# A four-layer decoder step: all convolution pairs from the fourth block on by seven products, with half of one low part made by an adding transfer

## The chip, the cores and the metric

The program runs on one core of a Trainium2 chip, in one launch. The metric is device microseconds, the median of several runs. Engines are named as in the profile: PE (TensorE), ACT (ScalarE), DVE (VectorE), POOL (GpSimd), and SP, which only issues transfers. PEld is PE's weight load.

## What is computed

One inference step of four layers, for 512 prompt tokens and 8 sample tokens that share all weights (520 columns; the model width is 1024). Each layer has another token mixer; the change is in layer 1, the gated short convolution:

```python
def shortconv_mixer(h, w_in, conv_w, w_out, buf):
    u = h @ w_in
    bg, cg, xb, z = jnp.split(u, 4, axis=-1)
    cx = cg * xb
    ...
    out = (bg * y * jax.nn.silu(z)) @ w_out
```

Here `w_in` is 1024 x 8192, so each of the four parts has 16 row blocks of 128. All arithmetic is float32 in effect.

## The kernel before

**Products in two halves.** Every weight tile (128 x 1024, 512 KB) is split into a high part, `h`, which PE's rounded format holds exactly, and a low part, `l`, the rest. A product is then three matmuls: high by high, high by low and low by high. ACT makes the high part (`high`, L253), DVE subtracts it from the tile (`low`, L262). For `w_b` and `w_bo`, the weights of this layer, the low part of a tile is made without DVE: ACT writes minus the high part (L258), and a transfer on POOL's queue adds the tile from memory to it (L260). The code calls this `moved`.

**Pairs by seven products.** A plain tile takes 48 matmuls of some 260 columns, so two take 96. `seven` (L341) computes two tiles at once by seven products in place of eight, 84 matmuls. It needs three sums of quarters of the tiles, S1, S2 and S4, each 128 x 512. POOL forms them (L277 to L280, operation `sum`), and writes the difference of the first halves over the second tile (L278). The sums are split like a tile (`hs`, `ls`). In a pair, PE goes through its parts in this order: first half of tile 1 ("11"), S2 ("T2"), S1 ("T1"), second half of tile 1 ("21"), then the product of the pair before that was left over (S4, "22", in `flush`), then the two halves of tile 2 ("T3", "T4"). Each is 12 matmuls. After "11" and "21" ACT copies a result out of PSUM (L377, L385); DVE adds the others (L380, L372, L389, L393).

**Which tiles.** The layer has 16 blocks `j` of four tiles each. `paired(j)` (L54) says how many of a block's two pairs go by seven products: none in the first three blocks, then two in even blocks and one in odd ones, so 6 x 2 + 7 x 1 = 19 pairs. In an odd block the other two tiles are plain. In each block the first pair gives `xb` and `cx`, the second `bg` and `z`. When the first pair's left-over is done, which is within the second pair, `first` runs: DVE multiplies `cx` (L1109), ACT scales it (`taps`, L1071), DVE adds the other taps (L1076 to L1079). Within the first pair of the next block `second` runs: SiLU on ACT, a product on DVE (L1115).

**What sets the order.** All engines work through their instructions in program order, and the program writes them by a plan. `due` gives every load, sum, high and low part a time on a planned clock, from the time at which PE is to use the tile; `pump` issues what is due, between PE's products. So an instruction that waits holds up everything behind it on its engine. Weight buffers: four each for `wf`, `wh`, `wl`, `hs` and `ls`.

The part of `due` for a pair, with `t` the planned start of the pair:

```python
one = at(max(ld, ld2, t - 12.8), i, "sum")
h1 = at(max(ld, take("wh", t + 5.76), t - 14.4), i, "high")
h2 = at(max(ld2, take("wh", t + 10.08), one + 6.6), i, "high2")
```

Of the kernel before, what the change touches and what calls it, by code (L numbers as in the profile page):

```python
# [10 lines left out]
AF = mybir.ActivationFunctionType  # L11
ALU = mybir.AluOpType
# [27 lines left out]
NPLAIN = 3  # L40
# [12 lines left out]

def paired(j):  # L54

    return 0 if j < NPLAIN else 2 - j % 2


def plan():
# [25 lines left out]
    for j in range(16):  # L85
        for n, q in enumerate(((2, 1), (0, 3))):
            keys = [("w_b", 16 * u + j) for u in q]
            if n < paired(j):
                out.append(Item(*keys, cost=10.08))
            else:  # L90
                out.extend(Item(key) for key in keys)
# [21 lines left out]
def due(items):  # L113

    ops, t, seq = [], 0.0, 0
    slots = {"wf": [0.0] * FBUFS, "wh": [0.0] * HBUFS, "hs": [0.0] * SBUFS}

    def take(tag, until):
        free = slots[tag]
        at = min(free)  # L120
        free.remove(at)
        free.append(until)
        return at

    def at(time, i, op):
        nonlocal seq
        ops.append((time, seq, i, op))
        seq += 1
        return time

    for i, it in enumerate(items):
        it.begin = t
        if len(it.keys) == 1:
            ld = min(slots["wf"])
            sp = at(max(ld, take("wh", t + (it.life or it.cost))), i, "split")
            at(take("wf", sp + 3) - 0.01, i, "load")
        else:
            ld, ld2 = sorted(slots["wf"])[:2]
# [3 lines that stand above are left out]
            low1 = at(h1 + 1.3 if it.moved else max(h1 + 1.3, one + 3), i, "low")  # L142
            low2 = at(max(h2 + 1.3, one + 3), i, "low2")
            at(take("wf", max(low1, one + 7) + 1) - 0.01, i, "load")
            at(take("wf", low2 + 3) - 0.01, i, "load2")
            for n, need, until in (("2", t - 4.6, t + 2.88), ("1", t - 3.4, t + 4.32), ("4", t - 1.4, t + 17.3)):
                h = at(max(take("hs", until), need, one + 3), i, "high" + "s" + n)
                at(h + 0.6, i, "lows" + n)
        t += it.cost
    return sorted(ops)  # L150


class Stream:
# [5 lines left out]
    def step(self):  # L159
        while self.gens:  # L160
            try:
                next(self.gens[0])
                return
            except StopIteration:
                self.gens.pop(0)
# [27 lines left out]
class Net:  # L193
    def __init__(self, ctx, tc, d):
        self.tc, self.nc, self.d = tc, tc.nc, d
        nc = self.nc
        ctx.enter_context(tc.manual_schedule())
        pool = lambda name, **kw: ctx.enter_context(tc.tile_pool(name=name, **kw))
        self.cp = pool("const", bufs=1)
        self.wp = pool("w", bufs=HBUFS)  # L200
        self.xp = pool("xres", bufs=1)
        self.ap = pool("act", bufs=49)
        self.pm = pool("pm", bufs=2, space=bass.MemoryType.PSUM)
        self.pa = pool("pa", bufs=4, space=bass.MemoryType.PSUM)
        self.dr = pool("scr", bufs=1, space=bass.MemoryType.DRAM)
        self.n = 0
        self.streams = []
        self.gate, self.finish, self.look = Gate(0.5), None, 0
        self.items = plan()
        self.ops, self.begun, self.made = due(self.items), 0, set()  # L210
        self.wt, self.wpos, self.clock, self.pend = {}, 0, 0.0, None

        self.cols = self.cp.tile([P, NCOL], F32, name="cols")
        self.eps = self.cp.tile([P, 1], F32, name="eps")
        self.onesd = self.cp.tile([P, P], F32, name="onesd")
        self.ident = self.cp.tile([P, P], F32, name="ident")
        self.ones = self.cp.tile([P, P], F32, name="ones")
        nc.vector.memset(self.eps, EPS)
        nc.vector.memset(self.onesd, 1.0 / 1024)
        nc.vector.memset(self.ones, 1.0)  # L220
        self.x = [self.xp.tile([P, T], F32, name=f"x{k}") for k in range(KD)]
# [19 lines left out]
    def make(self, i, op):  # L241

        if (i, op) in self.made:
            return
        self.made.add((i, op))
        nc, it = self.nc, self.items[i]
        t = self.wt.setdefault(i, {})
        f = lambda tile: tile.bitcast(F32)
        new = lambda tag, n=1024, pool=None, dt=F32R: (pool or self.wp).tile([P, n], dt, tag=tag, name=self.nm(tag))

        def high(k, tag, n=1024, pool=None):
            t["h" + k] = new(tag, n, pool)
            nc.scalar.activation(t["h" + k], t["w" + k], AF.Copy)  # L253

        def low(k, tag, n=1024, pool=None):
            t["l" + k] = new(tag, n, pool)
            if k == "1" and it.moved:
                nc.scalar.activation(t["l1"], f(t["h1"]), AF.Copy, scale=-1.0)  # L258
                key = it.keys[0]
                nc.gpsimd.dma_start(t["l1"], self.d[key[0]][key[1:]], accum_op=ALU.add)  # L260
                return
            nc.vector.tensor_sub(t["l" + k], t["w" + k], f(t["h" + k]))  # L262

        a, b = slice(0, 512), slice(512, 1024)
        sub = nc.gpsimd.tensor_sub
        if op in ("load", "load2"):
            n = 2 if op == "load2" else 1
            key = it.keys[n - 1]
            t[f"w{n}"] = self.wp.tile([P, 1024], F32, tag="wf", name=self.nm("wf"), bufs=FBUFS)
            nc.sync.dma_start(t[f"w{n}"], self.d[key[0]][key[1:]])  # L270
        elif op == "split":
            high("1", "wh")
            low("1", "wl")
        elif op == "sum":
            w1, w2 = t["w1"], t["w2"]
            s1, s2, s4 = (self.act()[:, :512] for _ in range(3))
            nc.gpsimd.tensor_add(s1, w2[:, a], w2[:, b])  # L277
            sub(w2[:, a], w1[:, a], w2[:, a])  # L278
            sub(s2, s1, w1[:, a])
            sub(s4, w1[:, b], s2)  # L280
            t.update(ws1=s1, ws2=s2, ws4=s4)
        else:
            k = op.removeprefix("high").removeprefix("low") or "1"
            step = high if op.startswith("high") else low
            if k[0] == "s":
                step(k, op[0] + "s", 512, self.sp)
            else:
                step(k, "w" + op[0])
# [763 lines left out]
    def conv(self, h, lay):  # L1052
# [4 lines left out]
        with ExitStack() as st:  # L1057
# [45 lines left out]
            def block(j):  # L1103
                xb, cx, z = (self.act() for _ in range(3))
                bg = self.act() if paired(j) > 1 else None
                c = []

                def first():
                    nc.vector.tensor_mul(cx, cx, xb)  # L1109
                    c.extend(taps(j, cx))  # L1110
                    conv(j, cx, *c)

                def second():
                    nc.scalar.activation(z, z, AF.Silu)
                    nc.vector.tensor_mul(c[0], bg, c[0])  # L1115
                    self.gate.gens.append(times(c[0], z))

                self.seven((("w_b", 32 + j), ("w_b", 16 + j)), self.sums, (xb, cx), first)
                if j == 15:
                    self.gate.drain()  # L1120
                    self.gate.gens.extend(parts(n) for n in range(4))
                if paired(j) > 1:
                    self.seven((("w_b", j), ("w_b", 48 + j)), self.sums, (bg, z), second)
                else:
                    ps = self.proj("w_b", j, a=h)
                    nc.vector.tensor_mul(c[0], ps, c[0])
                    ps = self.proj("w_b", 48 + j, a=h)
                    nc.scalar.activation(z, ps, AF.Silu)
                    self.gate.gens.append(times(c[0], z))
# [549 lines left out]
```

## Time and profile before

| what | us |
| --- | --- |
| median of 3 runs | 2178.26 |
| lowest, highest | 2176.53, 2182.1 |
| the profiled execution | 2174.19 |
| its span | 2172.4 |

The span is what the trace covers; 1.8 us lie around it. Blocks 3 to 15 of the convolution run from 679.46 to 957.30 us of the span. A timeline row gives start and duration in us, engine, line, operation, and in brackets the idle time before it with the instruction that ended it. Times of POOL instructions include what they wait for once begun. A matmul's duration (some 283 ns) is longer than the distance to the next, since matmuls are pipelined; the distance counts.

### The profile page before, as it was taken

To read this page: it belongs to the slowest core of one execution; us is meant where nothing else is said; L and a number is where in the kernel's file an instruction comes from. 1 tells how busy PE (TensorE), PEld (TensorE's weight loads), DVE (VectorE), ACT (ScalarE), POOL (GpSimd) and SP (SyncE) were. 2 spreads that over 40 slices of the span, in tenths; PEclk is the share of its full clock that TensorE was granted. 3 is DMA by queue.
4 is the path that set the end of the run, shared out by engine and by line. 5 is a ranking of instruction groups with operands and counts; after the bars stand their busy time and mean duration, and the time that the engine had idled before them with its cause. 6 is when DMAs were issued, how large, how long until landed. Compare 5 with 4: busy or idle time off the path is not lost.

```text
span 2172.4 us, 42676 instructions
## 1 busy us (share of the span) xinstructions
PE 2134.1 (98%) x17560; PEld 2112.8 (97%) x17560; DVE 1393.8 (64%) x3060; ACT 901.0 (41%) x1438; POOL 415.1 (19%) x491
## 2 busy tenths in 40 slices
PE   8999999999999999999999999999999999999998
PEld 8999999999999999999998999999999999999998
DVE  7676667653466766751477787787876566676434
ACT  6444454432465554554333333333335342322233
POOL 1101110100035545521014332232320000000000
PEclk9999999999999999999999999999999999999999
DMA  5644454332277666687233555455555233223421
GB/s 165 207 159 139 155 183 159 99 106 90 86 170 165 156 175 156 154 200 184 88 118 121 191 174 178 158 190 167 184 165 185 88 113 101 88 90 96 127 79 50
DMA packets 113527, 307.32 MB, mean 141 GB/s; under 512 B 34324, under 2 KB 38676, under 8 KB 111284
## 3 DMA queue, kind: packets, MB, share of 16 engines
q1 hardware_dynamic: 104404, 272.54, 38.2%
q0 software_dynamic: 8784, 31.99, 8.5%
q8 instruction: 138, 2.26, 0.4%
q14 instruction: 57, 0.47, 0.1%
q10 hardware_dynamic: 144, 0.06, 0.0%
HBM read 281.72 MB, written 22.82 MB: 140 GB/s over the span
## 4 chain that ended last, share of the span: by engine, by line
PE 80%; DVE 9%; issue 3%; ACT 3%; DMA 3%; POOL 1%; SPq 0%; DVEq 0%; ACTq 0%; POOLq 0%
PE ps L334 21%; PE ps L336 21%; PE ps L338 21%; PE ax L364 1%; DVE wl L262 1%; PE ax L362 1%; PE ax L363 1%; PE ax L334 1%; PE ax L338 1%; PE ax L336 1%; PE ps L362 1%; PE ps L363 1%; PE ps L364 1%; PE ax L1329 1%; DMA kc<-kc 1%
## 5 line engine op out<-in xcount | busy, mean ns | idle before, releaser
L334 PE MATMUL ps<-hi,wh 128*128 128x256 f32 x4672 | 964.0, 288 | 11.1 <-DVE a L485 7.1
L336 PE MATMUL ps<-lo,wh 128*128 128x256 f32 x4672 | 941.7, 283 | 1.0 <-DVE lo L800 0.8
L338 PE MATMUL ps<-hi,wl 128*128 128x256 f32 x4672 | 941.5, 283 | 0.6 <-DMA wl<-w_bo 0.4
L334 PEld LDWEIGHTS ps<-hi,wh 128*128 128x128 f32 x4672 | 727.2, 189 | 17.7 <-issue 7.4
L336 PEld LDWEIGHTS ps<-lo,wh 128*128 128x128 f32 x4672 | 725.9, 189 | 1.4 <-DVE lo L800 1.0
L338 PEld LDWEIGHTS ps<-hi,wl 128*128 128x128 f32 x4672 | 725.5, 189 | 1.0 <-DMA wl<-w_bo 0.6
L262 DVE TENSOR_TENSOR wl<-wf,wh 128x1024 fp32r<-128x1024 f32 x283 | 356.6, 1263 | 179.0 <-ACT wh L253 176.5
L253 ACT ACTIVATE wh<-wf 128x1024 fp32r<-128x1024 f32 x344 | 361.0, 1053 | 162.2 <-issue 86.3
L1207 POOL TENSOR_TENSOR a<-a,a 32x520 f32<-32x520 f32 x48 | 74.4, 1551 | 273.5 <-DVE a L485 101.8
L502 ACT ACTIVATE a<-ps 128x520 f32<-128x520 f32 x42 | 47.6, 1133 | 133.4 <-PE ps L338 112.2
L260 POOL DMA_DIRECT2D wl<-w_b x45 | 39.8, 884 | 327.4 <-ACT wl L258 308.1
L627 DVE TENSOR_TENSOR x<-ps,x 128x520 f32<-128x520 f32 x32 | 22.4, 699 | 122.8 <-PE ps L338 122.7
L1208 POOL TENSOR_TENSOR a<-a,a 32x520 f32<-32x520 f32 x48 | 66.3, 1382 | 144.6 <-DVE a L1206 98.5
L489 ACT ACTIVATE a<-a 128x520 f32<-128x520 f32 x42 | 26.8, 639 | 147.2 <-DVE a L485 147.1
L466 ACT ACTIVATE hi<-x 128x520 fp32r<-128x520 f32 x32 | 20.5, 639 | 156.9 <-DVE x L627 156.9
L485 DVE TENSOR_TENSOR a<-ps,a 128x520 f32<-128x520 f32 x85 | 59.0, 694 | 21.2 <-PE ps L338 17.8
L649 DVE TENSOR_TENSOR a<-ax,a 128x256 f32<-128x256 f32 (+1 forms) x62 | 23.7, 424 | 75.3 <-ACT a L647 75.3
L459 DVE CUSTOM_DVE_ANT_0 kc<-kc,qb 128x128 f32<-128x128 f32 (+1 forms) x192 | 58.0, 356 | 20.7 <-DMA kc<-kc 20.7
L1233 ACT ACTIVATE S<-S,nmx 128x128 f32<-128x128 f32 (+1 forms) x96 | 39.9, 417 | 72.3 <-DVE nmx L1230 72.3
L258 ACT ACTIVATE wl<-wh 128x1024 fp32r<-128x1024 f32 x61 | 64.6, 1058 | 1.6
L459 DVE CUSTOM_DVE_ANT_0 vc<-vc,pb 128x128 f32<-128x128 f32 (+1 forms) x192 | 61.8, 379 | 1.8 <-DMA pb<-scr_p 1.3
L262 DVE TENSOR_TENSOR ls<-a,hs 128x512 fp32r<-128x512 f32 x57 | 62.6, 1128 | 0.0
(344 smaller groups left out, 2890.5 us busy)
## 6 DMA issues: line engine op xcount, KB each, us to landing
wf<-w_c SPq DMA_DIRECT2D x80, 512.0 KB, 5.6
wf<-w_a SPq DMA_DIRECT2D x64, 512.0 KB, 3.7
wf<-w_b SPq DMA_DIRECT2D x64, 512.0 KB, 3.6
wl<-w_b POOLq DMA_DIRECT2D x45, 512.0 KB, 6.4
wf<-w_pg SPq DMA_DIRECT2D x32, 512.0 KB, 3.6
wf<-w_d SPq DMA_DIRECT2D x32, 512.0 KB, 3.4
pb<-scr_p SPq DMA_DIRECT2D x8, 1292.0 KB, 6.5
Ci<-C_in SPq DMA_DIRECT2D x16, 512.0 KB, 7.5
```

What stands on the lines that cost most here:

```text
L253: nc.scalar.activation(t["h" + k], t["w" + k], AF.Copy)
L258: nc.scalar.activation(t["l1"], f(t["h1"]), AF.Copy, scale=-1.0)
L262: nc.vector.tensor_sub(t["l" + k], t["w" + k], f(t["h" + k]))
L334: mm(out[j], wh, a[0][:, PARTS[j]], start=start, stop=False)
L336: mm(out[j], wh, a[1][:, PARTS[j]], start=False, stop=False)
L338: mm(out[j], wl, a[0][:, PARTS[j]], start=False, stop=stop)
L362: mm(out, w[0][:, c], hi, start=start and k == 0, stop=False, **go)
L459: self.nc.vector.tensor_tensor_reduce(junk, a, b, 1.0, 0.0, ALU.mult, ALU.add, out)
L485: nc.vector.tensor_mul(dst[:, :T], ps, self.r)
L502: nc.scalar.activation(dst, split(ps), AF.Copy)
L1207: nc.gpsimd.tensor_mul(b[:32], t[:32], cs[0])
L1208: nc.gpsimd.tensor_mul(a[:32], a[:32], cs[1])
```

## The change

Three edits. `paired` gives 2 for all blocks from the fourth on: 26 pairs by seven products, 7 more, and 14 fewer plain tiles. In the low part of a pair's second tile, the second half (columns 512 to 1023) is now made like the moved tiles: minus the high part by ACT (new L264), then an adding transfer of 256 KB on POOL's queue (new L266); DVE subtracts the first half only. And S2 is formed before the difference that goes over the second tile, with the planned times of the split sums moved ahead. All later lines are numbered 6 higher.

```diff
 def paired(j):
-    return 0 if j < NPLAIN else 2 - j % 2
+    return 0 if j < NPLAIN else 2
...
-            for n, need, until in (("2", t - 4.6, t + 2.88), ("1", t - 3.4, t + 4.32), ("4", t - 1.4, t + 17.3)):
+            for n, need, until in (("2", t - 6.8, t + 2.88), ("1", t - 4.8, t + 4.32), ("4", t - 2.0, t + 17.3)):
...
-            nc.vector.tensor_sub(t["l" + k], t["w" + k], f(t["h" + k]))
+            cols = slice(0, n)
+            if k == "2" and it.moved:
+                nc.scalar.activation(t["l2"][:, b], f(t["h2"][:, b]), AF.Copy, scale=-1.0)
+                key = it.keys[1]
+                nc.gpsimd.dma_start(t["l2"][:, b], self.d[key[0]][key[1:]][:, b], accum_op=ALU.add)
+                cols = a
+            nc.vector.tensor_sub(t["l" + k][:, cols], t["w" + k][:, cols], f(t["h" + k][:, cols]))
...
             nc.gpsimd.tensor_add(s1, w2[:, a], w2[:, b])
+            sub(s2, s1, w1[:, a])
             sub(w2[:, a], w1[:, a], w2[:, a])
-            sub(s2, s1, w1[:, a])
             sub(s4, w1[:, b], s2)
```

What the engines then find in a row, from the program before and the changed one, within the second pair of a block (of block 4 before, of block 4 after). In these rows `wf` is a loaded tile, `wh`/`wl` its high and low part, `hs`/`ls` those of a sum, `a` an activation tile or a sum, `ax` and `ps` PSUM.

ACT before, from the high part of the next pair's second tile on:

```order
L253 ACTIVATE wh_8413<-wf_8232 128x1024
L385 ACTIVATE a_8254<-ax_8370 128x260
L253 ACTIVATE hs_8432<-a_8358 128x512
L1071 ACTIVATE a_8450<-a_8252,cols 128x520
L253 ACTIVATE wh_8456<-wf_8316 128x1024
L258 ACTIVATE wl_8458<-wh_8456 128x1024
L253 ACTIVATE hs_8463<-a_8357 128x512
L253 ACTIVATE hs_8495<-a_8359 128x512
L253 ACTIVATE wh_8504<-wf_8364 128x1024
L258 ACTIVATE wl_8506<-wh_8504 128x1024
L377 ACTIVATE a_8512<-ax_8509 128x260
```

ACT after, from the same instruction:

```order
L253 ACTIVATE wh_8439<-wf_8241 128x1024
L391 ACTIVATE a_8261<-ax_8394 128x260
L264 ACTIVATE wl_8456<-wh_8439 128x512
L253 ACTIVATE hs_8462<-a_8367 128x512
L1077 ACTIVATE a_8480<-a_8259,cols 128x520
L253 ACTIVATE wh_8486<-wf_8328 128x1024
L258 ACTIVATE wl_8490<-wh_8486 128x1024
L253 ACTIVATE hs_8513<-a_8369 128x512
L383 ACTIVATE a_8539<-ax_8536 128x260
L253 ACTIVATE hs_8579<-a_8507 128x512
L253 ACTIVATE wh_8581<-wf_8376 128x1024
```

Behind L391 (before: L385) there now stand the negated half (L264), S1's high part, the taps, and the high and the negated high part of the pair after next (L253, L258); S2's high part has moved ahead of the second tile's, and two more pairs' parts follow where a block before had plain tiles.

POOL before, from one adding transfer to the next:

```order
L260 DMA wl_8339<-w_b 128x1024
L277 TENSOR_TENSOR a_8357<-wf_8232 128x512
L278 TENSOR_TENSOR wf_8232<-wf_8186,wf_8232 128x512
L279 TENSOR_TENSOR a_8358<-a_8357,wf_8186 128x512
L280 TENSOR_TENSOR a_8359<-wf_8186,a_8358 128x512
L1067 COPY cv_p<-a_8252 128x2
L1068 COPY cv_s<-a_8252 128x8
L260 DMA wl_8458<-w_b 128x1024
```

POOL after:

```order
L260 DMA wl_8351<-w_b 128x1024
L283 TENSOR_TENSOR a_8367<-wf_8241 128x512
L284 TENSOR_TENSOR a_8368<-a_8367,wf_8186 128x512
L285 TENSOR_TENSOR wf_8241<-wf_8186,wf_8241 128x512
L286 TENSOR_TENSOR a_8369<-wf_8186,a_8368 128x512
L266 DMA wl_8456<-w_b 128x512
L1073 COPY cv_p<-a_8259 128x2
L1074 COPY cv_s<-a_8259 128x8
L260 DMA wl_8490<-w_b 128x1024
```

S2 (L284) and the difference over the tile (L285) have changed places, and the transfer of the half (L266) stands between the sums and the copies.

DVE before, from the low part of the second tile on:

```order
L262 TENSOR_TENSOR wl_8428<-wf_8232,wh_8413 128x1024
L372 TENSOR_TENSOR a_8251<-ps_8257,a_8258 128x260
L1109 TENSOR_TENSOR a_8252<-a_8252,a_8251 128x520
L1076 SCALAR_TENSOR_TENSOR a_8450<-a_8252,cols,a_8450 128x511
L1077 SCALAR_TENSOR_TENSOR a_8450<-a_8252,cols,a_8450 128x510
L1078 SCALAR_TENSOR_TENSOR a_8450<-cv_in,cols,a_8450 128x8
L1079 SCALAR_TENSOR_TENSOR a_8450<-cv_in,cols,a_8450 128x8
L262 TENSOR_TENSOR ls_8461<-a_8358,hs_8432 128x512
```

DVE after, from S2's low part:

```order
L268 TENSOR_TENSOR ls_8441<-a_8368,hs_8437 128x512
L268 TENSOR_TENSOR wl_8456<-wf_8241,wh_8439 128x512
L378 TENSOR_TENSOR a_8258<-ps_8264,a_8265 128x260
L1115 TENSOR_TENSOR a_8259<-a_8259,a_8258 128x520
L1082 SCALAR_TENSOR_TENSOR a_8480<-a_8259,cols,a_8480 128x511
L1083 SCALAR_TENSOR_TENSOR a_8480<-a_8259,cols,a_8480 128x510
L1084 SCALAR_TENSOR_TENSOR a_8480<-cv_in,cols,a_8480 128x8
L1085 SCALAR_TENSOR_TENSOR a_8480<-cv_in,cols,a_8480 128x8
L268 TENSOR_TENSOR ls_8488<-a_8367,hs_8462 128x512
```

S2's low part now stands before L378 and L1115 and the taps; S1's, the last row, stays behind them (before, S2's stood there). The low part of the tile has 512 columns in place of 1024.

## Rows read from the trace of the kernel before

**Rows 1.** The page's part 1, busy time of each engine

```profile
PE 2134.1 (98%) x17560; PEld 2112.8 (97%) x17560; DVE 1393.8 (64%) x3060; ACT 901.0 (41%) x1438; POOL 415.1 (19%) x491
```

**Rows 2.** Stretches: length; busy us (count) of PE, PEld, DVE, ACT, POOL; clock, DMA

```profile
679.46:957.30 277.84, 274.67 (x2271) 272.67 (x2270) 186.38 (x243) 146.20 (x208) 143.37 (x132) 1.00 0.67 166
722.10:764.82 42.72, 42.17 (x348) 41.84 (x348) 30.41 (x39) 22.31 (x33) 23.79 (x22) 1.00 0.63 154
```

**Rows 3.** Timeline of PE, one stall, and the only group of the stage with idle time

```profile
722.10 0.39 PE L364 MATMUL ax<-ha,ls 128*128 128x260 f32 x1 [0.51 <-DVE ls L262]
...
L364 PE MATMUL ax<-ha,ls 128*128 128x260 f32 x76 | 22.1, 290 | 3.2 <-DVE ls L262 3.2
```

**Rows 4.** Timeline of ACT, end of one pair of tiles and start of the next

```profile
714.68 1.06 ACT L253 ACTIVATE wh<-wf 128x1024 fp32r<-128x1024 f32 x1 [2.96 <-POOL wf L278]
715.65 0.39 ACT L385 ACTIVATE a<-ax 128x260 f32<-128x260 f32 x1
715.96 0.63 ACT L253 ACTIVATE hs<-a 128x512 fp32r<-128x512 f32 x1
718.75 0.73 ACT L1071 ACTIVATE a<-a,cols 128x520 f32<-128x520 f32 x1 [2.16 <-DVE a L1109]
719.38 1.05 ACT L253 ACTIVATE wh<-wf 128x1024 fp32r<-128x1024 f32 x1
720.46 1.06 ACT L258 ACTIVATE wl<-wh 128x1024 fp32r<-128x1024 f32 x1
...
726.97 0.63 ACT L1114 ACTIVATE a<-a 128x520 f32<-128x520 f32 x1
727.49 1.05 ACT L253 ACTIVATE wh<-wf 128x1024 fp32r<-128x1024 f32 x1
...
751.97 1.05 ACT L258 ACTIVATE wl<-wh 128x1024 fp32r<-128x1024 f32 x1
...
757.41 1.06 ACT L253 ACTIVATE wh<-wf 128x1024 fp32r<-128x1024 f32 x1 [3.00 <-POOL wf L278]
```

**Rows 5.** Timeline of POOL, one set of sums; then line 279, ns minimum/median/maximum

```profile
753.42 0.91 POOL L260 DMA_DIRECT2D wl<-w_b  x1 [3.35 <-ACT wl L258]
754.04 1.62 POOL L277 TENSOR_TENSOR a<-wf 128x512 f32<-128x512 f32 x1
755.74 1.64 POOL L278 TENSOR_TENSOR wf<-wf,wf 128x512 f32<-128x512 f32 x1
757.32 1.30 POOL L279 TENSOR_TENSOR a<-a,wf 128x512 f32<-128x512 f32 x1
758.70 2.17 POOL L280 TENSOR_TENSOR a<-wf,a 128x512 f32<-128x512 f32 x1
...
L279 POOL TENSOR_TENSOR a<-a,wf x19: 1287/1299/1747, 671.5 to 928.2; 128x512 f32<-128x512 f32 x19
```

**Rows 6.** Timeline of DVE around those sums

```profile
758.50 1.23 DVE L262 TENSOR_TENSOR wl<-wf,wh 128x1024 fp32r<-128x1024 f32 x1 [1.94 <-ACT wh L253]
...
948.82 0.43 DVE L372 TENSOR_TENSOR a<-ps,a 128x260 f32<-128x260 f32 x1 [2.98 <-PE ps L364]
949.28 0.70 DVE L1109 TENSOR_TENSOR a<-a,a 128x520 f32<-128x520 f32 x1
950.78 0.75 DVE L1076 SCALAR_TENSOR_TENSOR a<-a,cols,a 128x511 f32<-128x511 f32 x1 [0.80 <-ACT a L1071]
...
952.63 0.69 DVE L1136 TENSOR_TENSOR lo<-a,hi 128x520 fp32r<-128x520 f32 x1
```

**Rows 7.** DVE and POOL at once: an instruction of eight columns; the same alone

```profile
673.26 1.34 DVE L1079 SCALAR_TENSOR_TENSOR a<-cv_in,cols,a 128x8 f32<-128x8 f32 x1
...
673.28 1.29 POOL L280 TENSOR_TENSOR a<-wf,a 128x512 f32<-128x512 f32 x1
...
952.49 0.23 DVE L1079 SCALAR_TENSOR_TENSOR a<-cv_in,cols,a 128x8 f32<-128x8 f32 x1
```

**Rows 8.** Part 6 of the page: adding transfers on POOL's queue, us to landing

```profile
wl<-w_b POOLq DMA_DIRECT2D x45, 512.0 KB, 6.4
```

## The prediction, made before the changed kernel ran

> **What bounds the kernel now.** I began with the page's busy times: PE is busy for 98% of the span [rows 1]. That alone does not say how near PE is to its floor, since matmuls are pipelined, so I went on to the stage that the change touches. From the first matmul of block 3 to the end of block 15 it takes 277.84 us, with TensorE at its full granted clock (1.00, the 2.4 GHz level) [rows 2]. From one of PE's stalls to the next, 42.72 us, lie two blocks: 168 matmuls of a double block and 180 of a mixed one, 348 in all, in 42.17 us of busy time, which is 0.1212 us from matmul to matmul [rows 2]. PE waits for one thing only in this stage: the low part of S2, 3.2 us in all, in the pair that is the third in a row [rows 3]. The other engines have room by their sums: of 277.84 us POOL is busy for 143, ACT for 146, DVE for 186 [rows 2]. So by shares PE is the bound, and a shorter list of matmuls is a gain. What the shares do not show is how ACT, POOL and DVE wait for each other, in order, and this is where I think the case is decided.
>
> **What PE gains.** A pair is 84 matmuls, 10.18 us, and each of its seven products 1.454 us. Seven pairs take the place of 14 plain tiles, 7 x (96 - 84) = 84 matmuls less, 84 x 0.1212 = 10.2 us. All 13 blocks are then 168 matmuls, 20.36 us each, 264.7 us. Against 277.84 that is a gain of 13.1 us, the stalls of before included. This is the floor that PE sets.
>
> **The loop of ACT and POOL.** Now I ask what a pair needs of the others when all pairs follow each other. In the changed order there is a ring that goes round once in each pair, and it holds no PE step that could make it wait once it is late. ACT writes the negated high part of a pair's first tile. POOL waits for it, in order, to issue the adding transfer, and only then begins that pair's sums. ACT's high part of the second tile waits for the difference that POOL writes over that tile; this is now the third of the sums and was the second. Behind that high part stand, on ACT, the copy L391, the negated half, S1, the taps or SiLU, and the high and negated high part of the next first tile, with which the ring closes. I call w the time at which the high part of the second tile starts, counted from PE's start of the pair that runs then.
>
> The POOL part: 753.02 (the end of the negated part that starts at 751.97) to 753.42 is 0.40 [rows 4, 5]; 0.62 to the first sum; three sums 754.04 to 758.62, 4.58; 0.03 to ACT, as from the end of L278 at 757.38 to 757.41 [rows 4, 5]. Together 5.63 us.
>
> The ACT part in a block's first pair, with SiLU: 0.97 for the high part and 0.31 for the copy (714.68, 715.65, 715.96), then three steps of 0.52, the negated half, S1 and SiLU (the step from 726.97 to 727.49, which has 520 columns), then 1.08 and 1.06 for the high and the negated part [rows 4]. Together 4.98 us. The negated half is new here, and the third sum came into the POOL part.
>
> The ACT part in a block's second pair, with the taps, is longer, because the taps wait for DVE. Before the taps DVE has to do the low part of S2, the first half of the tile's low part, L378 and L1115. Alone, the half would start 1.09 us after w (757.41 to 758.50 [rows 4, 6]) and take half of 1.23, 0.62. But POOL forms S4 just then, and the two do not run at once: an instruction of eight columns, 0.23 us alone, took 1.34 us and ended within 0.03 us of the sum that POOL had begun [rows 7]. So I count S2's low part 0.62, S4 1.29 and the half 0.62 in turn: 2.53 us. Then 0.46 for L378, 0.70 for the product, 0.04 to the taps, 0.63 for them (718.75 to 719.38), 1.08 and 1.06 [rows 4, 6]. Together 6.50 us.
>
> (The Trainium skill, page SBUF — State Buffer, section "Who interferes with whom", says that a VectorE instruction with two inputs in SBUF and a GpSimd instruction that reads SBUF hold one port by turns, for the whole instruction. The row above agrees. By this rule the sum is 2190 us, as below; if they overlapped freely it would be 2181.)
>
> One block is thus 4.98 + 6.50 + 2 x 5.63 = 22.74 us of the ring, against 20.36 of PE. The excess is **2.38 us per block**. Before, the mixed blocks hid this: a plain tile has no sums, and in each of them the ring caught up.
>
> **Where it reaches PE.** The tightest cover is the low part of S1. It stands on DVE behind the taps' four additions: 3.73 us from w to the taps, 0.76 until the first addition (950.02, the end of L1109 and 0.04, to 950.78), 1.85 for the four (to 952.63), 0.62 for itself, so it is there at w + 6.96 [rows 6]. The next pair's third product needs it at 10.18 + 2.91 + 0.24 = 13.33, so w may be 6.37. On time, L391 starts at 5.82 + 0.28 = 6.10, the ring closes 4.01 + 5.63 later at 15.74, and w is 5.56. The cover is 0.81 us and is gone in the first block. From then on PE stalls once a block, in the first pair of the next one. Over the 11 steps from the first to the twelfth of these transitions w grows by 26.2, to 31.7, 25.4 more than allowed. The stage takes 264.7 + 25.4 = 290.1 us, **12.2 us more** than 277.84.
>
> **The other edits.** The adding transfers cost POOL some 0.9 us each (753.42 has 0.91 [rows 5]); the new one stands behind the sums and before a wait for the taps that lasts longer, so I count it at nothing in the ring. Its landing is not in the trace; by the 512 KB transfers it is at most the 6.4 us of a whole tile [rows 8], at least half, 3.2. It starts about w + 2.4 and is needed at 19.15, so at w = 8.3 it has 2 us of cover. The first tile's transfer, at w + 6.9 with 6.4 us, is there at w + 13.3 for a need at 20.6, 0.9 us at w = 6.4; if it lasts longer PE waits for this, but the ring does not, so it shifts the end once, by a microsecond or two, and not per block. DVE loses 26 halves of 0.62 us; only the turns above matter. S2 a sum earlier, and its planned time moved ahead of the taps, takes away the 3.2 us of stalls for S2; this is in the floor. SP issues the same 64 loads, and nothing else of the program changes its work.
>
> **The sum.** The profiled execution took 2174.19 us, its span and 1.8 us around it, and the median of the runs is 4.1 above. 2174.19 + 12.2 = 2186.4, and on the median 2178.26 + 12.2 = 2190.5. I give 2190. The bounds of this case come from the sums: with the second and third at their least, 1.29, the three take 4.28, the excess is 1.78, and the time 2184; with the third at 1.75, its greatest [rows 5], the excess is 3.28 and the time 2200. So 2184 to 2200, if the ring holds.
>
> **Rivals.** First, *the ring is not what sets the pace* and PE runs at its floor: 2178.3 - 13.1 = 2165, faster. It would need a ring below 20.36, 2.4 us shorter a block than I sum. For it: before, in double blocks, ACT stood waiting for PE, and PE stalled only at the third pair. Against it: that third pair came late just because the taps waited 2.16 us for DVE [rows 4], which is a part of this ring. The point from which it decides is one: if any ACT row that I placed in the ring finds its inputs early enough to run while POOL sums. Second, *DVE and POOL overlap* where I take turns: then the half ends at w + 1.71, the second pair's part is 5.68, the excess 1.56, S1's cover 1.6; the growth over 11 steps is 17.2, the delay 15.5, the stage 280.2 and the time 2181, no change that can be told. For it: the trace of before has no S2 low part at this place. Third, *a ring with longer waits*, over 2200, if the adding transfers get slower with 26 more of them.
>
> **How the numbers follow.** The ring as summed 0.58, the floor 0.20, overlap 0.17, longer waits 0.05. A measurement of this kernel can tell about 0.3%, 6.5 us, so faster is below 2171.7 and slower above 2184.8. Faster: 0.20. Same: 0.17 and 0.03 of the ring's low end. Slower: 0.60. The forecast's own range is 2184 to 2200. As cases of other signs hold 0.37, the range reaches down to the floor case, 2165, which leaves half of that (0.10) and the 0.05 above 2200 out.
>
> **What would show it.** Right: PE idle in the stage some 25 us, in one stall of 2 to 3 us a block, ended by DVE's low part of a sum (L268), at PE's third product of a block's first pair; ACT's high part of second tiles waiting for POOL's L285 in every pair, and L391 starting late, right behind it; 22 to 23 us from block to block. Wrong: blocks 20.4 us apart, L391 on time and ACT idle before it. If the stalls are ended by a transfer instead, the ring is not the cause but the landing.

## The result: 11 us slower, and the profile after

The changed kernel takes 2187.84 us (median of 8 runs, 2184.14 to 2194.17) beside 2176.88 for the kernel before in the same session. The ratio is 1.0053, 95% interval 1.0038 to 1.0068: slower by 11.0 us. The profiled execution took 2186.68 us.

Four views of it, in the order in which I read them. First the page's busy times, to be laid beside [rows 1], and its chain of waits, by engine:

```profile
PE 2124.9 (97%) x17476; PEld 2100.4 (96%) x17476; DVE 1438.3 (66%) x3116; ACT 924.5 (42%) x1492; POOL 472.6 (22%) x538
PE 70%; DVE 8%; ACT 7%; POOL 6%; issue 6%; DMA 3%; SPq 0%; ACTq 0%; DVEq 0%; POOLq 0%
```

PE issues 84 matmuls less, as counted, and its share of the span falls. POOL, which one would call idle at 22% busy, holds 6% of the chain.

Then the changed stage, from the first matmul of block 3 to the end of block 15 (stretch: length; busy us and count of PE, PEld, DVE, ACT, POOL; clock, DMA), and what PE waited for in it (total us, times, longest):

```profile
680.40:975.10 294.70, 268.59 (x2185) 263.57 (x2185) 230.18 (x296) 170.28 (x264) 200.31 (x177) 1.00 0.72 168
```
```profile
PE ps L370 <- DVE ls L268: 13.2, 11, 1.2
PE ax L368 <- DVE a L386: 9.0, 11, 0.8
PE ps L368 <- DVE a L399: 2.7, 1, 2.7
PE ax L368 <- ACT a L383: 1.3, 1, 1.3
```

294.7 us against 277.84 [rows 2], and two waits that come eleven times each, where there had been one kind of wait, 3.2 us in all [rows 3]. The timeline of the weight loads shows their rhythm (start, duration, what; in brackets the idle time before):

```profile
724.73 0.19 PEld L370 LDWEIGHTS ps<-ha,ls 128*128 128x128 f32 x1 [1.40 <-DVE ls L268]
739.95 0.19 PEld L368 LDWEIGHTS ax<-hb,wh 128*128 128x128 f32 x1 [1.03 <-DVE a L386]
747.40 0.19 PEld L370 LDWEIGHTS ps<-ha,ls 128*128 128x128 f32 x1 [1.40 <-DVE ls L268]
762.63 0.19 PEld L368 LDWEIGHTS ax<-hb,wh 128*128 128x128 f32 x1 [1.03 <-DVE a L386]
770.09 0.19 PEld L370 LDWEIGHTS ps<-ha,ls 128*128 128x128 f32 x1 [1.41 <-DVE ls L268]
```

From 724.73 to 770.09 are two blocks: 22.68 us each. The forecast was 22.74, and 20.36 is what 168 matmuls take.

Last, the ring itself, in ACT's timeline from the high part of one pair's second tile to that of the next two:

```profile
797.78 1.06 ACT L253 ACTIVATE wh<-wf 128x1024 fp32r<-128x1024 f32 x1 [0.62 <-POOL wf L285]
...
800.59 1.04 ACT L253 ACTIVATE wh<-wf 128x1024 fp32r<-128x1024 f32 x1
801.66 1.06 ACT L258 ACTIVATE wl<-wh 128x1024 fp32r<-128x1024 f32 x1
...
807.06 0.63 ACT L253 ACTIVATE hs<-a 128x512 fp32r<-128x512 f32 x1 [3.54 <-POOL a L284]
808.75 1.06 ACT L253 ACTIVATE wh<-wf 128x1024 fp32r<-128x1024 f32 x1 [1.06 <-POOL wf L285]
...
812.09 0.73 ACT L1077 ACTIVATE a<-a,cols 128x520 f32<-128x520 f32 x1 [0.97 <-DVE a L1115]
812.73 1.05 ACT L253 ACTIVATE wh<-wf 128x1024 fp32r<-128x1024 f32 x1
813.81 1.06 ACT L258 ACTIVATE wl<-wh 128x1024 fp32r<-128x1024 f32 x1
...
820.46 1.06 ACT L253 ACTIVATE wh<-wf 128x1024 fp32r<-128x1024 f32 x1 [0.61 <-POOL wf L285]
```

and POOL's answer between 802.7 and 808.7, the same rows that in [rows 5] stood in before's order:

```profile
803.13 0.86 POOL L260 DMA_DIRECT2D wl<-w_b  x1 [2.20 <-ACT wl L258]
803.69 1.62 POOL L283 TENSOR_TENSOR a<-wf 128x512 f32<-128x512 f32 x1
805.39 1.63 POOL L284 TENSOR_TENSOR a<-a,wf 128x512 f32<-128x512 f32 x1
806.98 1.73 POOL L285 TENSOR_TENSOR wf<-wf,wf 128x512 f32<-128x512 f32 x1
```

ACT stands still for 3.54 and 1.06 us, for the sums that POOL may begin only when ACT has written the negated high part at 802.72; POOL in turn had stood still for 2.20, for ACT. ACT is busy for 58% of the stage and POOL for 68% (170.28 and 200.31 of 294.7), and each waits for the other. Over the whole stage, ACT's first wait and POOL's come to (total us, times, longest):

```profile
ACT hs L253 <- POOL a L284: 84.8, 24, 3.6
POOL wl L260 <- ACT wl L258: 64.9, 26, 2.8
```

The first half of the block is 808.75 - 797.78 = 10.97 us, the second 820.46 - 808.75 = 11.71.

### The profile page after: what moved, and what is told of

It reads as the page before. It is cut to its first block, busy times and chain, and to the rows that moved or that the text cites. A ratio compares the mean times of both kernels' runs of the same rounds, so it can differ in the third digit from the quotient of the medians.

```text
span 2184.6 us, 42744 instructions
## 1 busy us (share of the span) xinstructions
PE 2124.9 (97%) x17476; PEld 2100.4 (96%) x17476; DVE 1438.3 (66%) x3116; ACT 924.5 (42%) x1492; POOL 472.6 (22%) x538
## 4 chain that ended last, share of the span: by engine, by line
PE 70%; DVE 8%; ACT 7%; POOL 6%; issue 6%; DMA 3%; SPq 0%; ACTq 0%; DVEq 0%; POOLq 0%
PE ps L340 20%; PE ps L344 20%; PE ps L342 20%; ACT wh L253 3%; DVE wl L268 2%; POOL a L283 2%; POOL a L284 2%; POOL wf L285 2%; ACT wl L258 1%; PE ax L340 1%; PE ax L342 1%; PE ax L344 1%; PE ax L1335 1%; DMA kc<-kc 1%; POOL a L1214 1%
## 5 line engine op out<-in xcount | busy, mean ns | idle before, releaser
L340 PE MATMUL ps<-hi,wh 128*128 128x256 f32 x4448 | 917.8, 288 | 9.6 <-DVE a L491 7.3
L342 PE MATMUL ps<-lo,wh 128*128 128x256 f32 x4448 | 893.8, 282 | 0.1
L344 PE MATMUL ps<-hi,wl 128*128 128x256 f32 x4448 | 893.5, 282 | 0.4 <-DVE wl L268 0.3
L340 PEld LDWEIGHTS ps<-hi,wh 128*128 128x128 f32 x4448 | 690.7, 188 | 15.8 <-issue 7.6
L342 PEld LDWEIGHTS ps<-lo,wh 128*128 128x128 f32 x4448 | 689.6, 188 | 0.6 <-DVE lo L806 0.3
L344 PEld LDWEIGHTS ps<-hi,wl 128*128 128x128 f32 x4448 | 688.5, 188 | 0.8 <-DVE wl L268 0.5
L268 DVE TENSOR_TENSOR wl<-wf,wh 128x1024 fp32r<-128x1024 f32 (+1 forms) x290 | 357.4, 1236 | 180.1 <-ACT wh L253 177.0
L253 ACT ACTIVATE wh<-wf 128x1024 fp32r<-128x1024 f32 x344 | 361.4, 1053 | 158.8 <-issue 85.9
L268 DVE TENSOR_TENSOR ls<-a,hs 128x512 fp32r<-128x512 f32 x78 | 102.5, 1316 | 28.4 <-ACT hs L253 28.4
L260 POOL DMA_DIRECT2D wl<-w_b x38 | 33.3, 877 | 278.7 <-ACT wl L258 275.2
L253 ACT ACTIVATE hs<-a 128x512 fp32r<-128x512 f32 x78 | 48.5, 622 | 86.2 <-POOL a L284 86.2
L491 DVE TENSOR_TENSOR a<-ps,a 128x520 f32<-128x520 f32 x85 | 58.9, 693 | 21.0 <-PE ps L344 17.7
```

The costliest lines, as they stand in the source:

```text
L268: nc.vector.tensor_sub(t["l" + k][:, cols], t["w" + k][:, cols], f(t["h" + k][:, cols]))
L340: mm(out[j], wh, a[0][:, PARTS[j]], start=start, stop=False)
L342: mm(out[j], wh, a[1][:, PARTS[j]], start=False, stop=False)
L344: mm(out[j], wl, a[0][:, PARTS[j]], start=False, stop=stop)
L491: nc.vector.tensor_mul(dst[:, :T], ps, self.r)
```

## The experiments

Twelve kernels, each timed beside the kernel before; the ratio is to it, with its 95% interval. "Block" is read from the stalls of its trace as above; "stage" is the stretch of the thirteen blocks.

| kernel | median us | ratio | stage | block |
| --- | --- | --- | --- | --- |
| changed kernel | 2187.84 | 1.0053 (1.0038 to 1.0068) | 294.7 | 22.68 |
| ring_inside | 2220.56 | 1.0198 (1.018 to 1.0216) | 321.2 | 24.76 |
| ring_outside | 2193.07 | 1.008 (1.0063 to 1.0098) | 297.0 | 22.67 |
| sums_early | 2170.1 | 0.997 (0.9957 to 0.9983) | 267.2 | none |
| pairs_alone | 2176.36 | 0.9994 (0.9984 to 1.0005) | 278.3 | 21.24 |
| no_half | 2192.38 | 1.0066 (1.0046 to 1.0087) | 295.4 | 22.75 |
| old_sum_order | 2175.8 | 0.9994 (0.9978 to 1.001) | 276.2 | 21.13 |
| old_needs | 2201.0 | 1.0096 (1.008 to 1.0112) | 299.3 | 22.96 |
| early_after_two | 2167.94 | 0.9949 (0.9935 to 0.9964) | 270.3 | none |
| early_no_half | 2169.67 | 0.996 (0.9947 to 0.9973) | 272.3 | 20.69 |
| early_old_order | 2169.74 | 0.9959 (0.9945 to 0.9973) | 270.6 | none |
| pairs_sums_early | 2189.05 | 1.0051 (1.0035 to 1.0066) | 282.1 | 22.0 |
| early_pairs_alone | 2184.14 | 1.0021 (1.0012 to 1.0031) | 283.2 | 21.97 |

### Is it the ring? The same work inside it and outside

Two more copies of 128 x 512 a pair on ACT, whose result nothing reads. In the first kernel they stand between the high and the negated high part of the first tile, where I had drawn the ring; in the second behind S4's high part, outside (`if op == "highs4"`, with `t["ws4"]` copied).

```diff
             if k == "1" and it.moved:
+                if len(it.keys) == 2:
+                    for _ in range(2):
+                        nc.scalar.activation(self.act()[:, :512], f(t["h1"][:, :512]), AF.Copy)
                 nc.scalar.activation(t["l1"], f(t["h1"]), AF.Copy, scale=-1.0)
```

> The changed kernel with two more ACT copies of 128x512 (0.52 us each, into scratch) per pair, placed inside the ring, between the high and the negated high part of a pair's first tile. Ring: each block is 2 x 1.04 us longer, some 12 blocks late, +25 us: 2213 (2208 to 2216). If ACT has slack there, as its 42% busy time suggests, no change: 2188.

> The changed kernel with the same two ACT copies per pair, placed outside the ring: behind S4's high part, where ACT waits 3.5 us for POOL. Ring: no change, 2188 (2186 to 2190). If ACT's load counted, the same +25 us as inside.

The third product's stall, in the first and then in the second kernel:

```profile
756.83 0.19 PEld L373 LDWEIGHTS ps<-ha,ls 128*128 128x128 f32 x1 [1.41 <-DVE ls L271]
...
806.35 0.19 PEld L373 LDWEIGHTS ps<-ha,ls 128*128 128x128 f32 x1 [1.44 <-DVE ls L271]
```
```profile
748.89 0.19 PEld L373 LDWEIGHTS ps<-ha,ls 128*128 128x128 f32 x1 [1.42 <-DVE ls L268]
794.23 0.19 PEld L373 LDWEIGHTS ps<-ha,ls 128*128 128x128 f32 x1 [1.41 <-DVE ls L268]
```

Inside, a block takes (806.35 - 756.83) / 2 = 24.76 us, 2.08 more, which is four copies of 0.52. Outside it takes 22.67, as without them. ACT does the same extra work in both. So the ring sets the pace of a block, and a busier ACT doesn't. The totals came out larger than expected, by some 8 us inside and 3 to 7 outside: the blocks agree with the theory, the stage nearly (26.5 more inside, by 11 steps 23). The rest lies ahead of the stage, behind it, or in how it starts and ends, and what makes it is open.

### Breaking the ring: the sums planned earlier

```diff
-            one = at(max(ld, ld2, t - 12.8), i, "sum")
+            one = at(max(ld, ld2, t - 20.0), i, "sum")
```

> The changed kernel with one number altered: the sums of a pair are planned 20.0 us ahead of the pair in place of 12.8, so that POOL forms them one pair earlier and ACT's high part of the second tile no longer waits for them. The work of every engine is the same. If the ring of ACT and POOL (22.67 us a block in the trace after) sets the pace, it is cut and PE is back at its floor of 20.4 us a block: 2165 us (2162 to 2172). If the load of DVE or POOL, or their turns, set the pace, nothing changes: 2186 to 2190. If the transfers on POOL's queue do, likewise no gain.

One number changed, and the kernel is 17.7 us faster than the changed one. In the stage the wait at its end is the only one listed (second line), and two came in ahead of it (first line; what PE waited for from 640 to 960 us):

```profile
PE ps L340 <- DVE a L491: 4.5, 2, 3.1
PE ps L368 <- DVE a L399: 2.7, 1, 2.7
```

In ACT's timeline, with POOL's below it, the high part of a second tile now runs without a wait, since POOL had finished its last set of sums at 806.8 (second line):

```profile
811.67 1.05 ACT L253 ACTIVATE wh<-wf 128x1024 fp32r<-128x1024 f32 x1
...
805.08 1.74 POOL L286 TENSOR_TENSOR a<-wf,a 128x512 f32<-128x512 f32 x1
```

ACT's copy L391 now waits for PE in every pair, 49.4 us in 26 times, where in the changed kernel it did so twice, for 3.5: ACT is no longer late. DVE is busy for 238 us of this stage and POOL for 199, in 267 us, about as much as in the changed kernel (230 and 200), and DVE's low parts of sums are still stretched beside POOL's sums (1159 ns in the mean from 700 to 950 us, against 1344). So it is not their load that made the changed kernel slow, but the order. The gain is 5 us less than I had summed. The stage starts 9.1 us later than in the changed kernel (689.5 against 680.4); 4.5 of that are the two waits above, where the first early sums fall beside DVE's work for the last plain tiles, and the granted clock was 0.93 from 660 to 680 us, where it was 1.00 in the changed kernel. That this is what the 5 us went to is likely but not shown: early_after_two (below), with one wait of 1.4 in their place and one of 1.9 for a transfer, is only some 2 us faster.

### Which of the three edits closed the ring

The pairs alone, without the other two edits:

> The kernel before with the first edit alone: all 26 pairs by seven products, low parts and order of the sums as before. Ring: only two sums lie in it, and no negated half: first pair 4.95 + 4.35, second 7.35 + 4.35 (taps after the whole low part on DVE), 21.0 us a block against 20.4 of PE; stage some 271 us, 2170 (2166 to 2175), faster than before. If DVE's load is the bound, the whole low part on DVE (0.6 us more per pair) makes it slower than the changed kernel: over 2188.

No difference from the kernel before, and a miss: I had expected 2170. The matmuls saved are paid back by one stall a block, 21.24 us from one to the next against 21.0 summed, and the 2.7 us at the stage's end were not in my sum.

```profile
747.26 0.19 PEld L364 LDWEIGHTS ax<-ha,ls 128*128 128x128 f32 x1 [1.08 <-DVE ls L262]
789.74 0.19 PEld L364 LDWEIGHTS ax<-ha,ls 128*128 128x128 f32 x1 [1.07 <-DVE ls L262]
```

Then the changed kernel without the half transfer, with the sums and needed times of before, and with the needed times alone of before:

```diff
 # no_half
-            if k == "2" and it.moved:
+            if False:
 # old_sum_order, old_needs
-            for n, need, until in (("2", t - 6.8, t + 2.88), ("1", t - 4.8, t + 4.32), ("4", t - 2.0, t + 17.3)):
+            for n, need, until in (("2", t - 4.6, t + 2.88), ("1", t - 3.4, t + 4.32), ("4", t - 1.4, t + 17.3)):
 # old_sum_order alone: S2 third again
-            sub(s2, s1, w1[:, a])
             sub(w2[:, a], w1[:, a], w2[:, a])
+            sub(s2, s1, w1[:, a])
```

> The changed kernel, but the second tile's low part is formed whole by VectorE as before (no negated half on ScalarE, no half adding transfer); all pairs and S2 formed second stay. Ring: the pair next to a SiLU group loses the negated half (-0.52 us), the pair next to the taps gets the whole low part in front of them on VectorE (+0.6 us), so the block stays at 22.67 us (22.4 to 23.0) and the time within 2188 (2184 to 2191). Rival 'the half transfer is what costs' (22 more ScalarE copies and issues of 0.9 us on GpSimd): the loss of 11 us against the kernel with the pairs alone goes away, 2176 to 2180, with a block of 21.3 us or less.

> The changed kernel, but with S2 formed third and the sums' needed times of before; all pairs and the half adding transfer stay. Ring: the next tile's ScalarE high part waits for two GpSimd sums, not three; the negated half adds 0.52 us to the pair next to a SiLU group and the shorter VectorE low part takes about as much off the one next to the taps, so the block is that of the pairs alone, 21.25 us (21.0 to 21.6), and the time 2176 (2173 to 2181): the place of S2 would then hold the whole loss. Rival 'the half transfer costs': near 2188, block 22.3 us or more. If each holds a part: both this and the kernel without the half come out between 2179 and 2185.

> The changed kernel (sums 12.8 us ahead, half transfer, S2 formed second) with the needed times of before alone, so that S2's high part stands behind the second tile's high part on ScalarE, and S2's low part behind the second tile's half low part on VectorE. Ring: the second tile's high part still waits for three sums, so the pair next to a SiLU group stays at 10.97 us; the taps no longer have S2's low part (1.42 us) in front of them, so the pair next to the taps falls from 11.71 to about 10.8; block 21.8 us (21.5 to 22.1), time 2179 (2176 to 2184). Rival 'the place of S2 among the sums holds it all': block 22.67 and 2186 to 2190. Rival 'the needed times hold it all': block 21.25, 2174 to 2177.

Without the half transfer nothing comes back: block 22.75, 2192 (a little above the range expected). Its two halves of a block show why: the one with SiLU falls from 10.97 to 10.51 us, since ACT has no negated half to write, and the one with the taps grows from 11.71 to 12.24, since DVE subtracts the whole tile ahead of them. With S2 third again, and the needed times of before, all of it does: block (791.40 - 749.15) / 2 = 21.13, 2176.

```profile
749.15 0.19 PEld L370 LDWEIGHTS ax<-ha,ls 128*128 128x128 f32 x1 [0.94 <-DVE ls L268]
791.40 0.19 PEld L370 LDWEIGHTS ax<-ha,ls 128*128 128x128 f32 x1 [0.96 <-DVE ls L268]
```

So the loss stands with the place of S2 and the times that came with it: with S2 second the ring goes through three sums in place of two. S2 third with the new needed times was not run. The last kernel of the three was to say whether the needed times hold a share, and here I missed: I expected 2179 and it took 2201. Its trace shows why. With the needs of before, S1's high part falls between the first tile's high and negated high part, which is inside the ring (in the changed kernel these two stand next to each other, 800.59 and 801.66 above):

```profile
801.09 1.06 ACT L253 ACTIVATE wh<-wf 128x1024 fp32r<-128x1024 f32 x1 [4.78 <-POOL wf L285]
...
803.90 1.05 ACT L253 ACTIVATE wh<-wf 128x1024 fp32r<-128x1024 f32 x1
804.85 0.61 ACT L253 ACTIVATE hs<-a 128x512 fp32r<-128x512 f32 x1
805.36 1.05 ACT L258 ACTIVATE wl<-wh 128x1024 fp32r<-128x1024 f32 x1
...
812.43 1.06 ACT L253 ACTIVATE wh<-wf 128x1024 fp32r<-128x1024 f32 x1 [5.23 <-POOL wf L285]
...
824.04 1.06 ACT L253 ACTIVATE wh<-wf 128x1024 fp32r<-128x1024 f32 x1 [4.78 <-POOL wf L285]
```

824.04 - 801.09 = 22.95, the block of its stalls (22.96): the ring again, 0.27 longer. Eleven steps make 3 us of that, and the stage is 4.6 longer. The other 8 of the 13 us I can't place. The granted clock was 0.91 to 0.96 in four of ten 20 us slices read in its stage, and 1.00 in all of these in the changed kernel (below), but the stalls stay 22.9 to 23.0 us apart through them, so inside the stage the ring hides it. So the needs that came with the edit are a part of it that helps; moving S2 without them costs more.

### What is left once the ring is open

The first two pairs keep 12.8, so that their sums don't meet the last plain tiles, and all others have 20.0. Then the same without the half transfer, and the same with before's sum order and needs. Last, two kernels with the pairs alone, so without either edit: one with 20.0 for all pairs, and one that keeps 12.8 in the first two.

```diff
+    pairs = 0
...
+            pairs += 1
-            one = at(max(ld, ld2, t - 12.8), i, "sum")
+            one = at(max(ld, ld2, t - (20.0 if pairs > 2 else 12.8)), i, "sum")
```

> The changed kernel with the sums planned 20 us ahead from the third pair on, and 12.8 us ahead in the first two, whose early sums had met VectorE's work for the last plain tiles (1.42 and 3.12 us of idle TensorE there). Ring: both entry stalls go, one of 2.7 us at the start of the pairs may stay, stage 267 to 270, time 2167 (2163 to 2170). Rival 'the entry idle is the clock's or the stage's start, not the turns': 2170 to 2174, as with all sums early.

> The changed kernel with the sums planned 20 us ahead from the third pair on, and the second tile's low part whole on VectorE (no half transfer). Against the same early sums with the half transfer (2167.9), this one takes away the half alone. Theory: with the sums out of ScalarE's way VectorE is next, and 22 whole low parts (2.31 us each against 1.2 to 1.4 for a half) fill its queue; the T3 sum, which stands right behind the low part there, lets TensorE wait as in the kernel with early sums and pairs alone; stage 278 to 284, time 2183 (2177 to 2190). Rival 'it was the place of S2 and the needed times that the pairs alone lacked': stage 268 to 272, time 2168 (2164 to 2172).

> The changed kernel with the sums planned 20 us ahead from the third pair on, S2 formed third and the needed times of before; the half transfer stays. Theory: with early sums the place of S2 no longer matters, since nothing of ScalarE waits for a sum of the pair at hand; stage 268 to 273, time 2168 (2164 to 2172). Rival 'S2 second is needed there too': a stall before the S2 product once a pair, stage 276 or more, 2176 to 2188.

> The kernel before with every group in two pairs (the first edit alone) and the sums planned 20 us ahead of the pair's products instead of 12.8; no half transfer, S2 third. Ring: planned ahead, the sums leave ScalarE's way, the periodic stall (0.9 us before the S2 product) goes, stage 267 to 269 us, and the time is that of the changed kernel with early sums, 2169 (2165 to 2173). Rival 'the half transfer is needed once the ring is gone, since VectorE's low parts are late': a stall once a pair comes back, stage 273 or more, 2174 to 2180.

> The kernel before with every group in two pairs and the sums planned 20 us ahead from the third pair on, 12.8 us ahead in the first two; no half transfer, S2 third, needed times of before. It differs from the kernel with early sums and pairs alone (2189.1) in the first two pairs only, and from the two with early sums and one of the other edits (2169.7 each) by that edit. If it is the lack of both edits that fills VectorE's queue: the T3 sum waits behind whole low parts again, stage 278 to 284, time 2185 (2180 to 2191). If it was the start, where the early sums of the first two pairs met the last plain tiles and left VectorE behind for the blocks after: stage 269 to 274, time 2170 (2166 to 2174).

The first is the fastest kernel of the study, 2167.94, ahead of both kernels; from all sums early (2170.1) its interval doesn't set it clearly apart. With early sums one of the two other edits is enough: without the half, or without the new order, the time is 2170 in both, so my theory that the half alone relieves DVE was wrong. Without both it is 2184, and PE waits for DVE in eight blocks (here the kernel with pairs alone and early sums from the third pair):

```profile
742.66 0.19 PEld L364 LDWEIGHTS ax<-hb,wh 128*128 128x128 f32 x1 [1.75 <-DVE a L382]
764.63 0.19 PEld L364 LDWEIGHTS ax<-hb,wh 128*128 128x128 f32 x1 [1.80 <-DVE a L382]
```

Between these two, 21.97 us, DVE has no idle time but 0.80 us for the taps and 0.41 for PE: here DVE is the bound. What fills it is not more work, but longer instructions. The low parts of the sums from 700 to 950 us, in this kernel and then in the one that only lacks the half (busy us, mean ns):

```profile
L264 DVE TENSOR_TENSOR ls<-a,hs 128x512 fp32r<-128x512 f32 x70 | 90.7, 1295 | 0.0
```
```profile
L270 DVE TENSOR_TENSOR ls<-a,hs 128x512 fp32r<-128x512 f32 x71 | 75.1, 1058 | 0.0
```

As many instructions of the same shape, but for one, are 15.6 us apart. Those that lie beside no sum of POOL took 0.68 us each in both kernels (27 of the 70, 17 of the 71); those that do took 1.68 in the mean in the first and 1.18 in the second. So it is not how many of them meet a sum, but how long each then waits, and the work is the same in both: the order is what differs. The pairs alone with early sums from the first pair on had come out at 2189, where I had expected 2169. This kernel, with the first two pairs as before, was to say whether the start was to blame: it is for 5 to 7 of these 20 us (by the medians, or by the ratios).

## Why the prediction was right, point by point

- **The bound and its floor.** PE at 20.36 us a block was the right floor: with early sums the stage takes 267.2 us, about 264.7 and the 2.7 at its end. My rival "the ring doesn't pace", 2165, is near what the kernel becomes when the ring is open (2170.1, and 2167.9 at best).
- **The ring's sum.** 22.74 forecast, 22.68 measured; its place and its members were shown by the copies inside and outside. Two terms were off and cancel, which is luck. In the first pair POOL's part is 6.03 (802.72, the end of the negated part, to 808.75) against 5.63, since the third sum took 1.73 there and not 1.30 (5.02 from the first to the end of the third against 4.58). That is the slow case which my upper bound of 2200 set for both pairs; it came in one. In the second pair ACT's part is 6.12 (808.75 to 814.87) against 6.50: S2's low part had begun 0.9 us before the high part of the tile, so DVE reached the taps sooner, although S4 took 1.76 and not the 1.29 of the sum. I had put S2's low part behind.

```profile
807.84 1.42 DVE L268 TENSOR_TENSOR ls<-a,hs 128x512 fp32r<-128x512 f32 x1
809.84 1.14 DVE L268 TENSOR_TENSOR wl<-wf,wh 128x512 fp32r<-128x512 f32 x1 [0.58 <-ACT wh L253]
```

- **Turns of DVE and POOL.** They hold: the half of the low part took 1.14 beside S4's sum, against the 0.62 summed, and 0.69 where S4 was all but done when it began (at 802.19 in the kernel with before's needs). The rival that lets them overlap, 2181, is out.
- **Where PE stalls.** I said one stall of 2 to 3 us a block, at the third product of a block's first pair. There are two: that one, 1.2, ended by S1's low part as forecast (L268), and one of 0.8 at the sixth product of the block's second pair, for L386. On DVE, L386 stands behind S4's low part and a product of 520 columns, and both were stretched by POOL's sums; I had looked only at S1.

```profile
803.28 2.59 DVE L268 TENSOR_TENSOR ls<-a,hs 128x512 fp32r<-128x512 f32 x1 [0.46 <-ACT hs L253]
805.79 1.78 DVE L1089 TENSOR_TENSOR a<-a,a 128x520 f32<-128x520 f32 x1
807.50 0.41 DVE L386 TENSOR_TENSOR a<-ax,a 128x260 f32<-128x260 f32 x1
```

- **The stage.** Forecast 290.1, measured 294.7. Eleven steps of 22.68 - 20.36 make 25.5, near the 25.4 forecast. What the sum lacked is the end: the last pair's left-over product has no pair behind it to hide its wait, 2.7, and within that pair PE waits 1.3 for a copy of ACT (L383). Before, the last block ended in plain tiles. So the stage is 16.9 us longer than before, where I had 12.2. In these two profiles the time outside the stage fell by 4.4, which gives this back (12.5 between them, 11.0 between the medians); at 1180 to 1200 and 1380 to 1400 the profile of before had slices of a granted clock of 0.91 that the one after hadn't. No edit is behind the stage, yet the time there is anything from 1209.5 to 1216.4 us in the fourteen traces. I had no term for it, so that the total came out this near the forecast is in part luck; that the ring paces the blocks is not.
- **The other edits.** The issue of the half transfer costs the ring nothing that can be seen, as counted; the half as a whole gives to one half of the block what it takes from the other (10.51 and 12.24 without it). Its landing took 6.1 us in the median, near my upper end, and never ended a wait of PE. That S2's stall would go came true, but I counted the order of S2 as a gain of the floor alone. In fact it is the edit that costs: with S2 back in its place, and its planned times, the loss is gone. My prediction priced the third sum in the ring but did not say that without it the change would be even.

## What to carry to other kernels

When two engines with time to spare hand work to each other in program order, draw the ring and add it up per turn; it bounds the stage like a busy engine does. The shares don't show it; the lists of idle times show its waits, one on each engine (84.8 and 64.9 us above), but not that they close. Moving a producer's planned time by one turn opens such a ring without removing any work, so try that before moving work to another engine. It did not pay in every order: with the pairs alone, early sums made the kernel slower, since DVE then became the bound. And reckon an order by what stands between a wait and the instruction that the other engine waits for: one copy more there was 0.5 us a turn, the same copy behind it nothing.

## What the chip showed that I had not expected

The low part of a 128 x 512 sum, 0.68 us alone, took 2.59 us beside POOL's sums of 1.6 to 1.7 (the row at 803.28 above). The 1.91 us more are longer than the one sum that ran beside it to its end (1.62, from 803.69); what the rest waited for was not tried. And the granted clock: in the kernel with before's needs, whose PE stops for 2.4 us in most blocks, slices of 20 us fell to 0.91 in the middle of the stage, one of them shown here, with fewer matmuls in it than the same slice of the changed kernel, whose stops are 1.4 and 1.0 (length, PE busy and count, clock, DMA; first that kernel, then the changed one):

```profile
740.00:760.00 20.00, 17.66 (x133) 0.91 0.65 150
```
```profile
740.00:760.00 20.00, 18.82 (x155) 1.00 0.65 162
```

In the first of these slices the matmuls are 0.22 us apart from 750.67 to 753.48, behind the stop of 2.4 us that ends at 749.81, and 0.12 ahead of that stop and after 753.70, so they ran at the lower of the two levels there. The kernel without the half transfer, with stops of up to 1.9 us, had 0.91 in three of the ten slices; the one with copies inside the ring, with three stops of 1.4 to 1.5 us a block, had 1.00 in all ten. Whether the longer stops are the reason was not tried.
